# Two gate steps moved ahead of the first projections, and compressed scores in wider products

## The chip, the cores and the metric

The kernel runs on one core of one Trainium2 chip. The metric is the device time of one execution in microseconds (us). The kernel before takes 1661.98 us, the median of three runs (1661.27 to 1663.3).

## The reference, cut to what matters

The program computes a first block on 512 tokens of width 1024 and then two layers of a second block. The first block's attention is what the change touches. It has an mLSTM part (4 heads of 128) and a sparse attention part (8 heads of 64 in 2 groups), which are joined and multiplied by `w_out`.

```python
h = rms_norm(x, ln1_g)
mq, mk, mv, mo, mi, mf, aq, akc, avc, aks, avs, akw, avw, ag = split(h @ w_in)
# mLSTM: per head a row over the 512 tokens, from the two gate columns mi, mf
b = cumsum(log_sigmoid(mf + bias))          # a scan over the tokens
a = -b + (mi + bias)                        # then a running maximum of it
Wt = exp(D - m) * (q @ k.T);  hm = (Wt @ v) / max(|den|, exp(-m))
m_out = rms_norm(hm) * sigmoid(mo)
# sparse attention, branch 1 of 3: compressed keys, 32 per group
Kc, Vc = compress(akc), compress(avc)
p_c = softmax(q @ Kc.T - slope * dist);  o_c = p_c @ Vc
# branches 2 and 3: selected blocks and window, scores and values per head
a_out = g0 * o_c + g1 * o_s + g2 * o_w
x = x + concat(m_out, a_out) @ w_out
x = x + conv_ffn(rms_norm(x));  x = x + sigmoid(rms_norm(x) @ w_ple_gate) * (p @ w_ple_proj)
```

All of it is float32.

## The kernel before, in words

A float32 product is built from two reduced-precision parts of each operand, a high part (`whi`, `hh`) and a low part (`wlo`, `hl`). Three matmuls make one product: high by high, low by high, high by low (`mm`, lines 173 to 175). ScalarE (ACT) casts the high part of a weight tile (`split_w`, line 137). GpSimd (POOL) or VectorE (DVE) subtracts it from the raw tile to get the low part (lines 147 and 140). Activations are split likewise by `split`: ACT in line 201, DVE in line 202. SyncE (SP) issues the weight DMAs into `wraw` (line 157).

The first block's attention is written as a list of steps, `B1_ORDER`. `b1_attention` runs through it and emits each step's instructions. A scheduler then places them, and each engine runs its own queue in that order. The steps that matter here are:

- `B0`, `B1` (`b1_blocks`): key and value blocks for the compression. `v` (`b1_v`): values and gate columns (`gi`, line 784), 96 matmuls of 288 columns.
- `g` (`b1_gates`): 8 transposes of `gi` on TensorE (PE, line 663) and two biased copies on ACT (line 664) make the two gate rows, 4 partitions by 512 tokens.
- `R` (`b1_mlstm_rows`, lines 924 to 960): from these rows a chain over DVE and ACT: minimum (929), exp and log (930, 931), subtract (932), scan (934), subtract (937), scan with maximum (938), add (939), exp (940), a high part `m8` (945), and 4 transposes of the result on PE (line 954). Exp and log are in different activation tables, so that ACT loads a table in between (`ACT_TABLE_LOAD`).
- `Q` (`b1_mlstm_qk`): a projection with 24 matmuls of 512 columns; `k` and `q` are two and one more of these. `O` and `V`: mLSTM output gate (`mo`) and values. `M` (`b1_mlstm_head`): one mLSTM head, which ends in 4 transposes of `num` (line 1070).
- `S` (`b1_cmp_scores`): compressed scores of one group, for 4 token tiles and 4 heads. For each it has two matmuls of 32 columns, one with the high and one with the low part of the compressed keys `kc`, summed in one PSUM bank: 32 matmuls (line 838). One DVE addition of the bias (line 841) empties the bank, and the softmax follows.
- `A`, `P`, `E`: scores (line 878), transposes (901), values (907, 916) of the sparse heads.
- `u` (`b1_pT`): loads and transposes the second input (`praw`, line 632). `w` splits the first two mLSTM heads' outputs, and `W` (`b1_out`) multiplies them by their rows of `w_out`.

PSUM banks come from small pools. Projections, `S` and the transposes of `g` and `R` use the pool `psd`, which has two banks.

Of the kernel before, what the change touches and what calls it, by code (L numbers as in the profile page):

```python
# [9 lines left out]
OP = mybir.AluOpType  # L10
# [5 lines left out]
NT = 4  # L16
# [12 lines left out]
def sub(t, part, npart, off, dims):  # L29

    pitch = t.ap[0][0]
    return bass.AP(tensor=t.tensor, offset=t.offset + part * pitch + off,
                   ap=[[pitch, npart]] + [list(d) for d in dims])
# [7 lines left out]
class Build:  # L41
# [402 lines left out]

    B1_SIZES = dict(k=13, v=1, pa=6, pb=2, mp=6, p2=3, f=2, mf=2, ms=2)
    B1_D = (7,)
    B1_ORDER = "C B0 v B1 Q11 k q0 q1 Q00 X0 X1 g A00 O0 Y0 V0 A10 P00 Y1 S0 A01 A02 Q01 R M0 P01 P02 T0 A03 P03 A12 q2 E0 A11 P10 A13 P11 P12 P13 A30 E1 A20 P20 A21 P21 O1 q3 A22 A23 P22 Q10 A60 P23 V1 E2 A31 S1 P30 P31 A32 T1 A33 P32 M1 c Q21 A40 A42 Q20 P33 u E3 P40 A41 P41 A43 Q30 P42 A50 P43 w E4 W0 A52 P50 A51 P51 P52 A53 P53 A61 E5 A62 Q31 W1 P60 P61 M2 M3 A70 A63 P70 P62 P63 A72 U0 A71 A73 P71 P72 P73 U1 E6 E7"

    def b1_attention(self, ctx, h, first):
        self.c1 = self.pool(ctx, "const1", 1)  # L450
# [4 lines left out]
        self.aT, mT, x = [None] * 4, [None] * 4, {}  # L455
        for step in self.B1_ORDER.split():
            n = [int(c) for c in step[1:]]
# [366 lines left out]
    def b1_cmp_scores(self, g):  # L824

        nc, a = self.nc, self.a
        cbias = self.T("f", [128, NT, 128], name="cbias")
        nc.sync.dma_start(cbias, a["c_cbias"][g])
        pc = self.T("f", [128, NT, 128], name="pcx")
        mn = self.smallE([128, NT, 4], "cmn")  # L830
        ls = self.smallE([128, NT, 4], "cls")
        s = self.bankD()
        for i in range(NT):
            for r in range(4):
                hd = 4 * g + r
                lhs = self.qs[hd // 2][:, hd % 2, i * 128:(i + 1) * 128]
                for p in range(2):
                    nc.tensor.matmul(s[:, i * 128 + r * 32:i * 128 + r * 32 + 32], lhs,
                                     self.kc[:, p, 32 * g:32 * g + 32], start=(p == 0), stop=(p == 1))
        pf = pc.rearrange("p i (r n) -> p i r n", r=4)  # L840
        nc.vector.tensor_tensor(pc, s.rearrange("p (i n) -> p i n", i=NT), cbias, op=OP.add)
        nc.vector.tensor_reduce(mn, pf, axis=AX.X, op=OP.min)
        nc.vector.tensor_tensor(pf, sub(mn, 0, 128, 0, [[4, NT], [1, 4], [0, 32]]), pf, op=OP.subtract)
        nc.scalar.activation(pc, pc, AF.Exp)
        nc.vector.tensor_reduce(ls, pf, axis=AX.X, op=OP.add)
        nc.vector.reciprocal(ls, ls)
        nc.vector.tensor_tensor(ls, ls, sub(self.gate, 0, 128, 12 * g, [[24, NT], [3, 4]]), op=OP.mult)
        nc.vector.tensor_tensor(ls, ls, sub(self.rmask, 0, 128, 0, [[1, NT], [0, 4]]), op=OP.mult)
        nc.vector.tensor_tensor(pf, pf, sub(ls, 0, 128, 0, [[4, NT], [1, 4], [0, 32]]), op=OP.mult)
        return pc  # L850
# [937 lines left out]
```

## Time and profile before

| | us |
|---|---|
| median of 3 runs | 1661.98 |
| profiled execution | 1657.95 |
| its span (first to last instruction) | 1656.2 |
| PE busy / weight loads (PEld) | 1561.4 / 1385.7 |
| DVE / ACT / POOL busy | 943.6 / 756.2 / 546.9 |

The first block's attention lies between 20 and 335 us of the span; the rest is its dense part and the second block, which the change does not touch. PE is busy for 94% of the span, and the mean granted clock of TensorE is 0.98. The clock is told per stretch as a share of its upper level, 2.4 GHz; 0.50 is the lower one, 1.2 GHz. In such a table a busy time is followed by the number of instructions in brackets. A matmul's own time includes its way through the array, so that successive matmuls overlap: their spacing is read from the starts.

### The profile page before, as it was taken

How to read it: one execution, taken by the hardware profiler on the slowest of the kernel's cores; microseconds unless marked ns; L12 is line 12 of the kernel's file. 1: busy time of each engine (PE TensorE's matmuls, PEld its weight loads, DVE VectorE, ACT ScalarE, POOL GpSimd, SP SyncE). 2: the span in 40 equal slices, each digit the busy share in tenths (PEclk: the TensorE clock that was granted, in tenths of full speed). 3: DMA queues.
4: the chain of work that ended last, by engine and by line, in shares of the span. 5: the costliest groups of instructions: out<-in, count | busy, mean ns of one | idle time of the engine just before them, and what ended most of it. 6: DMA issues, size and time to landing. Idle time of an engine off the chain costs nothing.

```text
span 1656.2 us, 25923 instructions
## 1 busy us (share of the span) xinstructions
PE 1561.4 (94%) x9702; PEld 1385.7 (84%) x9702; DVE 943.6 (57%) x2090; ACT 756.2 (46%) x1703; POOL 546.9 (33%) x721
## 2 busy tenths in 40 slices
PE   6999998899999999898999999999989998999997
PEld 5899977778888888688899899998788786988785
DVE  4386667754454334646865558535447748566453
ACT  4465656743333323534554546533425545554432
POOL 4663533131111112347433243011666430431022
PEclk9999999999999999989999999999999999999999
DMA  5532222454333333322132144135322231333252
GB/s 173 139 103 68 65 77 83 161 179 153 100 89 101 103 105 112 104 75 65 39 83 69 54 124 121 40 120 164 115 61 64 78 90 38 102 111 93 73 182 76
DMA packets 189377, 163.61 MB, mean 99 GB/s; under 512 B 9664, under 2 KB 161312, under 8 KB 189252
## 3 DMA queue, kind: packets, MB, share of 16 engines
q1 hardware_dynamic: 189252, 161.96, 32.6%
q8 instruction: 76, 1.25, 0.3%
q14 instruction: 49, 0.40, 0.1%
HBM read 139.19 MB, written 12.58 MB: 92 GB/s over the span
## 4 chain that ended last, share of the span: by engine, by line
PE 72%; DVE 11%; DMA 5%; POOL 4%; ACT 4%; issue 3%; SPq 0%; POOLq 0%; DVEq 0%; ACTq 0%
PE psd L173 13%; PE psd L174 13%; PE psd L175 13%; PE pss L173 7%; PE pss L174 6%; PE pss L175 6%; POOL wlo L147 2%; DMA wraw<-in_w_in_dram 2%; ACT whi L137 2%; PE pss L1432 1%; PE pso L1469 1%; PE pst L1457 1%; DVE pt L202 1%; PE pss L1570 1%; DMA wraw<-in_w_out_dram 1%
## 5 line engine op out<-in xcount | busy, mean ns | idle before, releaser
L147 POOL TENSOR_TENSOR wlo<-wraw,whi 128x256 fp32r<-128x256 f32 (+1 forms) x432 | 320.7, 773 | 345.2 <-ACT whi L137 326.6
L137 ACT CAST whi<-wraw 128x1024 fp32r<-128x1024 f32 (+2 forms) x215 | 210.9, 981 | 332.0 <-PE pss L174 78.9
L173 PE MATMUL psd<-hh,whi 128*128 128x264 f32 (+2 forms) x1016 | 339.0, 335 | 2.9 <-DVE pT L202 1.2
L174 PE MATMUL psd<-hl,whi 128*128 128x264 f32 (+2 forms) x1016 | 338.5, 333 | 0.0
L175 PE MATMUL psd<-hh,wlo 128*128 128x264 f32 (+2 forms) x1016 | 337.2, 332 | 0.5 <-DVE wlo L140 0.5
L140 DVE TENSOR_TENSOR wlo<-wraw,whi 128x1024 fp32r<-128x1024 f32 (+1 forms) x106 | 116.0, 1094 | 189.5 <-ACT whi L137 189.2
L173 PEld LDWEIGHTS psd<-hh,whi 128*128 128x128 f32 x1016 | 192.6, 190 | 22.3 <-DVE pT L202 1.6
L175 PEld LDWEIGHTS psd<-hh,wlo 128*128 128x128 f32 x1016 | 192.7, 190 | 17.7 <-DVE wlo L140 1.0
L174 PEld LDWEIGHTS psd<-hl,whi 128*128 128x128 f32 x1016 | 192.8, 190 | 16.7
L173 PE MATMUL psd<-whi,hh 128*128 128x256 f32 (+1 forms) x480 | 140.2, 293 | 16.3 <-DVE va L202 11.3
L175 PE MATMUL psd<-whi,hl 128*128 128x256 f32 (+1 forms) x480 | 138.1, 288 | 0.0
L174 PE MATMUL psd<-wlo,hh 128*128 128x256 f32 (+1 forms) x480 | 138.0, 289 | 0.0
L173 PEld LDWEIGHTS psd<-whi,hh 128*128 128x128 f32 x480 | 92.8, 194 | 18.9 <-DVE va L202 12.2
L330 POOL TENSOR_TENSOR y<-x,g 128x512 f32<-128x512 f32 (+1 forms) x34 | 46.8, 1390 | 141.1 <-DVE x L522 102.1
L174 PEld LDWEIGHTS psd<-wlo,hh 128*128 128x128 f32 x480 | 93.0, 194 | 0.1
L175 PEld LDWEIGHTS psd<-whi,hl 128*128 128x128 f32 x480 | 93.0, 194 | 0.1
L201 ACT CAST pt<-pst 128x512 fp32r<-128x512 f32 (+3 forms) x130 | 63.7, 505 | 64.2 <-PE pst L1457 51.0
L202 DVE TENSOR_TENSOR pt<-pst,pt 128x512 fp32r<-128x512 f32 (+3 forms) x130 | 74.8, 582 | 22.8 <-ACT pt L201 22.1
L1115 POOL TENSOR_TENSOR act<-conv,act 128x512 fp32r<-128x512 f32 x16 | 25.4, 1588 | 163.6 <-ACT act L1114 163.6
L1441 ACT ACTIVATE pr<-pss,gls 128x528 f32<-128x528 f32 (+1 forms) x66 | 46.2, 700 | 47.7 <-DVE gls L1440 46.1
L1440 DVE TENSOR_REDUCE gls<-pss 128x1 f32<-128x528 f32 (+1 forms) x66 | 46.4, 703 | 37.4 <-PE pss L1432 36.6
L175 PE MATMUL pss<-hh,wlo 128*128 128x512 f32 x160 | 63.3, 396 | 0.0
(468 smaller groups left out, 3628.6 us busy)
## 6 DMA issues: line engine op xcount, KB each, us to landing
wraw<-in_w_in_dram SPq DMA_DIRECT2D x108, 512.0 KB
wraw<-in_w_up_dram SPq DMA_DIRECT2D x32, 512.0 KB
wraw<-in_w_out_dram SPq DMA_DIRECT2D x24, 512.0 KB
wraw<-in_w_down_dram SPq DMA_DIRECT2D x16, 512.0 KB
nbias<-in_na_bias_dram SPq DMA_DIRECT2D x16, 408.0 KB
k<-k SPq DMA_DIRECT2D x16, 296.0 KB
wraw<-in_w_ple_gate_dram SPq DMA_DIRECT2D x8, 512.0 KB
x_mid<-x SPq DMA_DIRECT2D x8, 512.0 KB
```

The costliest lines, as they stand in the source:

```text
L137: nc.scalar.copy(hi, raw)
L140: nc.vector.tensor_sub(lo, raw, hi.bitcast(F32))
L147: nc.gpsimd.tensor_sub(lo[:, p[0], p[1]], raw[:, p[0], p[1]], hi[:, p[0], p[1]].bitcast(F32))
L173: m(ps, A[0], B[0], start=start, stop=False)
L174: m(ps, A[0], B[1], start=False, stop=False)
L175: m(ps, A[1], B[0], start=False, stop=stop)
L201: nc.scalar.copy(hi, src)
L202: nc.vector.tensor_sub(lo, src, hi.bitcast(F32))
L330: self.nc.gpsimd.tensor_tensor(y[:n, c], x[:, c], g[:n, c], op=OP.mult)
L1115: nc.gpsimd.tensor_sub(lo, u, hi.bitcast(F32))
L1440: nc.vector.tensor_reduce(mx, sv, axis=AX.XY, op=OP.max, negate=True)
L1441: nc.scalar.activation(pr.rearrange("p (a n) -> p a n", a=2), sv, AF.Exp, bias=mx, accum_out=l)
```

## The change

`B1_ORDER` is another list, and `b1_cmp_scores` is written differently. Of the list, in the order of the new one:

- `g` and `R` stand before and after `B1`, right behind `v` and ahead of the projection `Q11`; they stood behind `X1` and behind `Q01`.
- `u` stands behind `A41`, not ahead of `E3`.
- `M2` stands behind `A50`, `M3` behind `P53`; both stood behind `P61`.
- `w` stands behind `A51`, `W0` behind `A53`, `W1` behind `P61`; they stood around `E4` and behind `Q31`. `Q31` stands behind `P50`.

A group's compressed scores become 16 matmuls of 64 columns in two banks, 8 in each. Both key parts lie side by side in the columns, and nothing is summed in PSUM. DVE adds the two halves: four additions of 256 columns (two per bank) in place of one of 512.

```diff
--- before.py
+++ after.py
@@ -444,7 +444,7 @@
 
     B1_SIZES = dict(k=13, v=1, pa=6, pb=2, mp=6, p2=3, f=2, mf=2, ms=2)
     B1_D = (7,)
-    B1_ORDER = "C B0 v B1 Q11 k q0 q1 Q00 X0 X1 g A00 ... S0 A01 A02 Q01 R M0 ... P33 u E3 P40 A41 P41 A43 Q30 P42 A50 P43 w E4 W0 A52 P50 A51 P51 P52 A53 P53 A61 E5 A62 Q31 W1 P60 P61 M2 M3 A70 ..."
+    B1_ORDER = "C B0 v g B1 R Q11 k q0 q1 Q00 X0 X1 A00 ... S0 A01 A02 Q01 M0 ... P33 E3 P40 A41 u P41 A43 Q30 P42 A50 M2 P43 E4 A52 P50 Q31 A51 w P51 P52 A53 W0 P53 M3 A61 E5 A62 P60 P61 W1 A70 ..."
 
     def b1_attention(self, ctx, h, first):
         self.c1 = self.pool(ctx, "const1", 1)
@@ -829,16 +829,19 @@
         pc = self.T("f", [128, NT, 128], name="pcx")
         mn = self.smallE([128, NT, 4], "cmn")
         ls = self.smallE([128, NT, 4], "cls")
-        s = self.bankD()
-        for i in range(NT):
-            for r in range(4):
-                hd = 4 * g + r
-                lhs = self.qs[hd // 2][:, hd % 2, i * 128:(i + 1) * 128]
-                for p in range(2):
-                    nc.tensor.matmul(s[:, i * 128 + r * 32:i * 128 + r * 32 + 32], lhs,
-                                     self.kc[:, p, 32 * g:32 * g + 32], start=(p == 0), stop=(p == 1))
+        rows = lambda t, b: t[:, 2 * b:2 * b + 2].rearrange("p i (r n) -> p (i r) n", r=4)
+        for b in range(2):
+
+            s = self.bankD()
+            for j in range(8):
+                i, hd = 2 * b + j // 4, 4 * g + j % 4
+                nc.tensor.matmul(s[:, 64 * j:64 * j + 64].rearrange("p (q n) -> p q n", q=2),
+                                 self.qs[hd // 2][:, hd % 2, i * 128:(i + 1) * 128],
+                                 self.kc[:, :, 32 * g:32 * g + 32], start=True, stop=True)
+            sv = s.rearrange("p (j q n) -> p j q n", j=8, q=2)
+            nc.vector.tensor_tensor(rows(pc, b), sv[:, :, 0], rows(cbias, b), op=OP.add)
+            nc.vector.tensor_tensor(rows(pc, b), sv[:, :, 1], rows(pc, b), op=OP.add)
         pf = pc.rearrange("p i (r n) -> p i r n", r=4)
-        nc.vector.tensor_tensor(pc, s.rearrange("p (i n) -> p i n", i=NT), cbias, op=OP.add)
         nc.vector.tensor_reduce(mn, pf, axis=AX.X, op=OP.min)
         nc.vector.tensor_tensor(pf, sub(mn, 0, 128, 0, [[4, NT], [1, 4], [0, 32]]), pf, op=OP.subtract)
         nc.scalar.activation(pc, pc, AF.Exp)
```

How the change moves instructions is seen in each engine's queue. A row gives the line, the operation, out<-in and the size, xN for repeats, and in brackets the engines or queues it waits for. Behind line 850 a line number of the changed kernel is 3 higher than before.

First PE's queue of the kernel before at the end of `v`, whose last matmuls write `psd` from `whi` and `hl`. Line 686 transposes a position table (`per`) for `B1`, and `hh`, `whi` with 512 columns is the projection `Q11`.

```order
L173 MATMUL psd<-whi,hh 128x288
L174 MATMUL psd<-wlo,hh 128x288
L175 MATMUL psd<-whi,hl 128x288
L686 MATMUL psd<-ident,per 128x128 [waits DMAHW3_49,DVE_49]
L173 MATMUL psd<-hh,whi 128x512 [waits DVE_49,Activation_49]
L174 MATMUL psd<-hl,whi 128x512
```

The same place of PE's queue in the changed kernel:

```order
L175 MATMUL psd<-whi,hl 128x288
L663 MATMUL psd<-ident,gi 4x128 [waits DVE_49]
L663 MATMUL psd<-ident,gi 4x128 x2
L663 MATMUL psd<-ident,gi 4x128 [waits Activation_49]
L663 MATMUL psd<-ident,gi 4x128 [waits DVE_49]
L663 MATMUL psd<-ident,gi 4x128 x3
L686 MATMUL psd<-ident,per 128x128 [waits DMAHW3_49,Activation_49]
L957 MATMUL psd<-ident,rows 128x128 [waits PE_49,Activation_49]
L957 MATMUL psd<-ident,rows 128x128 x3
L173 MATMUL psd<-hh,whi 128x512
L174 MATMUL psd<-hl,whi 128x512
```

The first transposes of the gate columns and the last ones of the finished rows now both stand between `v` and `Q11`.

ACT's queue of the changed kernel behind `v`: `cx` is the split of `B1`'s blocks, `lf` and `m` belong to `R`, `whi` is a weight tile of the coming projections.

```order
L664 ACTIVATE mif<-psd,gbias 4x512 [waits PE_49]
L201 CAST cx<-cxg 128x4x32 [waits DVE_49]
L201 CAST cx<-cxg 128x4x32 x3
L954 CAST onehot<-ohraw 128x4 [waits DMAHW5_49]
L201 CAST cx<-cxg 128x4x32 [waits DVE_49]
L201 CAST cx<-cxg 128x4x32 x3
L933 ACTIVATE lf_610<-lf_610 4x512 [waits DVE_49]
L137 CAST whi<-wraw 128x1024 [waits DMAHW6_49,Activation_49,Pool_49]
L934 ACT_TABLE_LOAD
L934 ACTIVATE lf_610<-lf_610 4x512 [waits Activation_49]
L948 CAST m_622<-mM 4x512 [waits DVE_49]
L943 ACT_TABLE_LOAD
```

The steps of `R` stand one behind the other here, with one weight cast among them, and both table loads with them.

PE's queue of the kernel before around the first group's compressed scores (line 838), with the sparse heads' scores (878) and transposes (901) and the projection `Q01` behind them:

```order
L838 MATMUL psd<-kc,qs 128x32 [waits DMAHW5_49]
L838 MATMUL psd<-kc,qs 128x32 x25
L878 MATMUL pss_1819<-k,qs 128x384 [waits DVE_49]
L878 MATMUL pss_1824<-k,qs 128x512 [waits DVE_49]
L901 MATMUL pst<-ident,sb 128x128 [waits DVE_49,PE_49]
L173 MATMUL psd<-hh,whi 128x512 [waits DVE_49]
```

In the changed kernel:

```order
L838 MATMUL psd<-kc,qs 128x64 [waits DMAHW6_49]
L838 MATMUL psd<-kc,qs 128x64 x4
L904 MATMUL pst<-ident,sb 128x128 [waits DVE_49,PE_49]
L881 MATMUL pss_1896<-k,qs 128x128 [waits DVE_49]
L881 MATMUL pss_1901<-k,qs 128x256 [waits DVE_49]
L838 MATMUL psd<-kc,qs 128x64 [waits DVE_49,PE_49]
L838 MATMUL psd<-kc,qs 128x64 x7
L904 MATMUL pst<-ident,sb 128x128 [waits DVE_49]
L173 MATMUL psd<-hh,whi 128x512 [waits DVE_49]
```

The second half now waits for DVE, and so does `Q01` behind it: both halves and `Q01` stand in the same one of the two `psd` banks, while the other is held by `Y1`, the compressed values.

## Rows read from the trace of the kernel before

**Rows 1.** The chain of waits that ended last, by engine.

```profile
PE 72%; DVE 11%; DMA 5%; POOL 4%; ACT 4%; issue 3%; SPq 0%; POOLq 0%; DVEq 0%; ACTq 0%
```

**Rows 2.** Busy table, most of the stage: stretch, PE, PEld, DVE, ACT, POOL, clock, DMA.

```profile
50.00:350.00 300.00, 280.33 (x1712) 247.31 (x1711) 194.72 (x561) 172.91 (x471) 122.03 (x171) 0.95 0.35 109
```

**Rows 3.** Timeline of PE behind step v: start, length, instruction, idle before and releaser.

```profile
47.74 0.27 PE L686 MATMUL psd<-ident,per 128*128 128x128 f32 x1
48.37 0.47 PE L173 MATMUL psd<-hh,whi 128*128 128x512 f32 x1 [0.36 <-DVE pet L688]
```

**Rows 4.** Timeline of ACT, same place.

```profile
48.37 0.15 ACT L784 COPY gi<-psd 128x8 f32<-128x8 f32 x1
...
49.83 0.90 ACT L201 CAST cx<-cxg 128x128 fp32r<-128x128 f32 x4 [1.03 <-DVE cxg L695]
...
55.56 1.05 ACT L137 CAST whi<-wraw 128x1024 fp32r<-128x1024 f32 x1 [3.43 <-DMA wraw<-in_w_in_dram]
```

**Rows 5.** Timeline of DVE, same place.

```profile
48.26 2.93 DVE L695 TENSOR_TENSOR cxg<-ks,pet 128x512 f32<-128x512 f32 x2
...
52.08 3.77 DVE L202 TENSOR_TENSOR cx<-cxg,cx 128x128 fp32r<-128x128 f32 x8
```

**Rows 6.** Groups by line, 85 to 150 us: busy, mean ns, idle before.

```profile
L938 DVE TENSOR_TENSOR_SCAN mM<-rows 4x512 f32<-4x512 f32 x1 | 1.2, 1240 | 0.0
L937 DVE TENSOR_TENSOR rows<-rows,lfF 4x512 f32<-4x512 f32 x1 | 0.9, 936 | 0.0
L841 DVE TENSOR_TENSOR pcx<-psd,cbias 128x512 f32<-128x512 f32 x1 | 0.7, 691 | 0.0
L945 ACT CAST m<-mM 4x512 fp32r<-4x512 f32 x1 | 0.6, 618 | 2.8 <-DVE mM L938 2.8
```

**Rows 7.** Timeline of ACT around the table load of step R.

```profile
100.94 1.28 ACT L931 ACT_TABLE_LOAD   x1
102.23 0.63 ACT L931 ACTIVATE lf<-lf 4x512 f32<-4x512 f32 x1
102.88 1.28 ACT L359 ACT_TABLE_LOAD   x1
```

**Rows 8.** What PE waited for, 104 to 335 us: total, times, longest.

```profile
PE psm L1070 <- DVE num L1068: 5.8, 1, 5.8
PE psd L173 <- ACT mo L359: 2.3, 1, 2.3
PE psd L173 <- DVE mq L205: 1.3, 1, 1.3
PE psd L173 <- DVE pT L202: 1.2, 1, 1.2
PE pss L173 <- ACT cat L212: 1.2, 1, 1.2
...
PE psd L632 <- DMA praw<-in_p_dram: 0.9, 1, 0.9
PE psd L173 <- ACT k L212: 0.9, 1, 0.9
```

**Rows 9.** Busy table, stretches of low clock.

```profile
104.00:108.00 4.00, 3.33 (x16) 3.33 (x17) 4.00 (x9) 1.81 (x7) 2.35 (x4) 0.57 0.46 131
131.00:137.00 6.00, 6.00 (x29) 5.60 (x29) 5.42 (x14) 1.78 (x8) 2.41 (x3) 0.56 0.57 169
330.00:336.00 6.00, 3.97 (x11) 2.96 (x12) 4.12 (x10) 3.70 (x7) 0.04 (x1) 0.50 0.84 329
```

**Rows 10.** Timeline of PE, 64-column matmuls and the first compressed scores.

```profile
127.50 0.27 PE L174 MATMUL psd<-w,grep 128*128 128x64 f32 x1
127.61 0.28 PE L175 MATMUL psd<-w,grep 128*128 128x64 f32 x1
...
129.03 4.56 PE L838 MATMUL psd<-kc,qs 128*128 128x32 f32 x32
```

More of the change, by code (lines that the diff above doesn't have):

```diff
@@ L446 @@
     B1_D = (7,)
-    B1_ORDER = "C B0 v B1 Q11 k q0 q1 Q00 X0 X1 g A00 O0 Y0 V0 A10 P00 Y1 S0 A01 A02 Q01 R M0 P01 P02 T0 A03 P03 A12 q2 E0 A11 P10 A13 P11 P12 P13 A30 E1 A20 P20 A21 P21 O1 q3 A22 A23 P22 Q10 A60 P23 V1 E2 A31 S1 P30 P31 A32 T1 A33 P32 M1 c Q21 A40 A42 Q20 P33 u E3 P40 A41 P41 A43 Q30 P42 A50 P43 w E4 W0 A52 P50 A51 P51 P52 A53 P53 A61 E5 A62 Q31 W1 P60 P61 M2 M3 A70 A63 P70 P62 P63 A72 U0 A71 A73 P71 P72 P73 U1 E6 E7"
+    B1_ORDER = "C B0 v g B1 R Q11 k q0 q1 Q00 X0 X1 A00 O0 Y0 V0 A10 P00 Y1 S0 A01 A02 Q01 M0 P01 P02 T0 A03 P03 A12 q2 E0 A11 P10 A13 P11 P12 P13 A30 E1 A20 P20 A21 P21 O1 q3 A22 A23 P22 Q10 A60 P23 V1 E2 A31 S1 P30 P31 A32 T1 A33 P32 M1 c Q21 A40 A42 Q20 P33 E3 P40 A41 u P41 A43 Q30 P42 A50 M2 P43 E4 A52 P50 Q31 A51 w P51 P52 A53 W0 P53 M3 A61 E5 A62 P60 P61 W1 A70 A63 P70 P62 P63 A72 U0 A71 A73 P71 P72 P73 U1 E6 E7"
     def b1_attention(self, ctx, h, first):
```

## The prediction

> **What bounds the kernel now.** I read the chain of waits first: 72% of it is PE and 11% DVE [rows 1]. So an edit is worth what it does to PE's queue, and an engine beside PE counts only where PE waits for it. The busy table then shows where PE is not full. From 50 to 350 us, most of the first block's attention, PE is busy for 280.33 of 300 us at a mean granted clock of 0.95 [rows 2]. That leaves 19.7 us of idle time and up to 15 us (5% of 300) lost to low clock, and all that a new order can win lies in these two. PE's waits name the places: 5.8 us for the last head's `num` in front of the dense part, 2.3 for `mo`, 1.3 and 0.9 around `W0` (`mq`, `k`), 1.2 and 0.9 in step `u` (`pT`, `praw`), 1.2 for `cat` [rows 8]. Behind or around such places the clock is at about half [rows 9]. Of the gate steps that are moved, little shows as a wait: their chain over DVE and ACT runs beside projections that keep PE busy. That is the point on which the forecast turns: before, the chain has cover; now PE stands in it.
>
> The sum is made against the profiled execution, 1657.95 us, which is 4.03 below the median of 1661.98. What comes out is added to the median.
>
> **g and R ahead of Q11.** PE executes its queue in the written order, and the four transposes of the finished rows now stand ahead of `Q11`. They need the last exp of the chain. So all of `g` and `R` is a wait of PE, with the projection and all behind it. Before, `Q11` starts at 48.37 us [rows 3]. The walk from there, with an estimated 0.1 us for a hand-over and durations from the rows:
>
> - The last `gi` copy on ACT ends at 48.52 (48.37 + 0.15) [rows 4]. Five transposes (four of the second row, the last of the first) at 0.11 spacing [rows 10] and one run through the array (0.27 as for `per` [rows 3]) bring PE to 49.3. The two biased copies on ACT are of the 4 by 512 kind. The eleven of that kind on the path take from 618 to 1240 ns, first and last in [rows 6], and add to 8.8 us. Two of the short ones bring ACT to 50.6.
> - DVE has the two `cxg` additions in its queue ahead of the first step of `R`: 2.93 us [rows 5], from about 50.3, since their `per` transpose stands behind those of `gi`. They end at 53.35, and the minimum at 54.05.
> - ACT: exp to 54.9; a `whi` cast of 1.05 [rows 4] stands ahead of the table load, to 56.0 (its weights landed at 55.56 before, which fits); table load 1.28 [rows 7], to 57.3; log to 57.95. Meanwhile DVE does the eight `cx` subtractions, 3.77 us [rows 5], to about 58.5.
> - DVE: subtract to 58.8, scan to 60.05, subtract 0.94 to 61.0, scan 1.24 to 62.2 [rows 6]. ACT: `m8` 0.62 [rows 6] to 62.85, the second table load 1.28 [rows 7] to 64.15 (it stands behind `m8`, so nothing hides it), exp to 64.8. PE: four transposes to 65.35.
>
> `Q11` starts 17.0 us later. If the hand-overs overlap as closely as neighbours on one engine do, 1.5 us less; with 0.25 us at each of twelve, about 3 more: 15.5 to 20. Nothing wins it back later as far as I see: the next five projections are PE's own work, and weights that are ready earlier don't shorten it.
>
> PE restarts at low clock. Between 104 and 108 us, behind the 2.3 us wait, PE is busy for 3.33 us at 0.57 [rows 9]; at full clock that is 1.90, so 1.4 is lost. Between 330 and 336, behind the longest wait, 3.97 at 0.50 loses 2.0. Between the two: +1.7.
>
> What goes at the old places: the wait for `pet`, 0.36 [rows 3], since `per` is ready long before; the wait for `mo`, 2.3 [rows 8], which ends late because ACT loads two tables just ahead of it [rows 7], and with it the 1.4 of low clock; twelve transposes at 0.11 [rows 10], 1.3. Together -5.4. Net of this part: 17.0 + 1.7 - 5.4 = +13.3.
>
> The Trainium skill weighs on one term. Its page "ScalarE: Activation LUTs", section "What ACT_TABLE_LOAD costs", gives about 1283 ns for the load and another 1380 ns of drain for each switch of set. The trace has the 1.28 us but not the drain: the log starts at 102.23, 0.01 us after the load ends at 102.22. By the page two switches would add 2.8 us to the stall and the forecast would be 1673.0; I go by the rows.
>
> **Compressed scores.** 32 matmuls take 4.56 us [rows 10], 0.1425 each; 16 take 2.3, so -2.3 a group. From 131 to 137 us, around the first group, PE is busy all 6.00 us, at 0.56 [rows 9]: 2.6 us (6.00 x 0.44) of low clock. If the clock stayed up, a group would give -4.9. Against it: PE's queue shows the second half and `Q01` behind it waiting for DVE, since both halves and `Q01` use one bank. An addition of 512 columns took 0.69 [rows 6]; the two waits cost up to 1.4. If a further clock fall comes with them (1.4 as above), a group costs +0.5 with the saved matmuls, or +2.8 if these were hidden anyway. I take -2.3 + 1.4 = -0.9 a group, -1.8 in all, from -9.8 to +5.6.
>
> **u later.** Its transposes of `praw` stand closer together, and the loads come through two buffers. The waits seen were 0.9 for the load and 1.2 for `pT` [rows 8]. Two such pairs at most are new: 0 to +4.2, and I take +2.5, a little over one pair, because the matmuls that stood between the transposes are what moved away.
>
> **w and W0 later.** The waits for `k` and `mq`, 0.9 + 1.3 [rows 8], go, because other matmuls now stand between the split and the product: -2.2. With the low clock behind them (1.4) it could be -3.6, or 0 if the new place has its own wait.
>
> **M2, M3 and the end.** Before, PE ends its work and waits 5.8 for `num` and 1.2 for `cat` [rows 8], 7.0 in all, then runs 2.0 us worth of low clock. Now twelve matmuls of 512 columns stand behind the last head's products, ahead of its transposes. Each takes between 0.11 [rows 10] and 0.47 [rows 3]; at 0.3 they cover 3.6 us: -3.6. Its bounds are 0 (the head is simply as late) and -9.0 (waits and clock all gone).
>
> **Sum.** 13.3 - 1.8 + 2.5 - 2.2 - 3.6 = +8.2: 1666.2 for the profiled execution, 1670.2 for the median.
>
> **Rivals.**
> - *The clock stays up.* A cause outside the counted work: PE at its upper level through `S`, `W0`, the restart and the end. Then each group gives -4.9 (8.0 better), the restart costs nothing (1.7 better), the end and `W0` gain 2.0 and 1.4: 13.1 in all, +8.2 becomes -4.9, 1657.1, faster. It decides once 11.5 of the 13.1 come (8.2 + 3.3); at 8.2 it makes no change. For it: all these stretches have low clock now, and fewer waits stand in them. Against: a 17 us wait is just what preceded the low clock in two of the three rows.
> - *The chain is paid back.* The eleven operations (8.8 us) leave a stretch in which DVE was busy for 4.00 of 4.00 us [rows 9]. If DVE and ACT set the pace from there to the first scores, all of it comes back: -0.6, 1661.4, no change. Against: in those rows PE is the one that is full wherever it does not wait for `mo`, which is already counted.
> - *The banks decide.* Both groups cost +2.8 and `u` its full 4.2: +9.1 on the sum, 1679.3. For it: one bank serves both halves and the projection.
> - *The wait is not there*, because PE's matmuls don't stand behind the rows' transposes on the chip. Then 18.7 go from the sum: -10.5, 1651.5. No row shows a matmul that starts ahead of a waiting one.
>
> **How the numbers follow.** The forecast has 0.42, the clock 0.17, the pay-back 0.20, the banks 0.15, no wait 0.06. A difference under 0.2% (3.3 us) can't be told from none here. So faster 0.23, same 0.20, slower 0.57. The range of 8 in 10 goes from 1655, which takes in most of the clock's case and leaves out the missing wait, to 1679, which leaves out half of the banks' case; the forecast's own range is 1666 to 1675.
>
> **What would show it.** In the profile after: PE idle for 15 to 20 us behind the 96 matmuls of `v`, released by ACT, with both table loads within the gap; then a clock near 0.5 for some 3 us. No wait for `mo` at `O0`. Twice 8 matmuls of 64 columns for each group, the second 8 released by DVE. Waits for `praw` of 2 us or more together. The wait for `num` at 2 to 3 us. I am wrong in the main point if `Q11` starts before 60 us, and wrong in the sum if the gap is there and the time is still below 1662: then the stretch from `Q11` to the dense part must be at least 17 us shorter, and the table of busy time and clock will say by which of the two.

## The result and the profile after

The changed kernel takes 1688.01 us, the median of four runs (1683.11 to 1690.39), against 1661.62 for the kernel before beside it. The ratio is 1.0163, 95% interval [1.0145, 1.0181]: slower by 26.4 us, where +8.2 was forecast and 1679 was the end of the range.

The wait that the forecast turns on is there. PE's timeline behind step `v` in the changed kernel, to set beside [rows 3] (start, length, instruction, idle time before it and its releaser):

```profile
49.03 0.27 PE L686 MATMUL psd<-ident,per 128*128 128x128 f32 x1
64.50 1.12 PE L957 MATMUL psd<-ident,rows 128*128 128x128 f32 x4 [15.19 <-ACT rows L943]
65.27 0.78 PE L173 MATMUL psd<-hh,whi 128*128 128x512 f32 x1
65.84 0.63 PE L174 MATMUL psd<-hl,whi 128*128 128x512 f32 x1
```

`Q11` starts at 65.27 in place of 48.37, 16.9 us later. ACT's timeline of the same stretch shows the chain that holds it; [rows 4, 7] are its counterparts:

```profile
54.00 1.03 ACT L137 CAST whi<-wraw 128x1024 fp32r<-128x1024 f32 x1
55.05 1.28 ACT L934 ACT_TABLE_LOAD   x1
56.34 0.63 ACT L934 ACTIVATE lf<-lf 4x512 f32<-4x512 f32 x1
61.89 0.62 ACT L948 CAST m<-mM 4x512 fp32r<-4x512 f32 x1 [4.92 <-DVE mM L941]
62.52 1.28 ACT L943 ACT_TABLE_LOAD   x1
63.82 0.63 ACT L943 ACTIVATE rows<-lfF 4x512 f32<-4x512 f32 x1
```

Both loads stand in the gap, and ACT goes on 0.01 and 0.02 us after each. The Trainium skill's page "ScalarE: Activation LUTs", section "What ACT_TABLE_LOAD costs", adds a drain of about 1380 ns to each switch. These rows show none, as [rows 7] did not.

The busy table of the stretch (PE, PEld, DVE, ACT, POOL, clock, DMA), before first, gives what PE loses:

```profile
48.00:70.00 22.00, 21.14 (x91) 16.81 (x91) 10.51 (x17) 9.71 (x22) 17.45 (x24) 1.00 0.50 134
```

```profile
48.00:70.00 22.00, 6.26 (x21) 4.94 (x21) 12.23 (x22) 9.25 (x19) 12.07 (x12) 0.62 0.26 73
```

The spacing of the matmuls is 0.43 until 70.1 us and 0.23 from there:

```profile
69.68 0.62 PE L174 MATMUL psd<-hl,whi 128*128 128x512 f32 x1
70.11 0.43 PE L175 MATMUL psd<-hh,wlo 128*128 128x512 f32 x1
70.61 0.39 PE L174 MATMUL psd<-hl,whi 128*128 128x512 f32 x1
70.84 0.39 PE L175 MATMUL psd<-hh,wlo 128*128 128x512 f32 x1
```

So the first 4.8 us of `Q11` run at the lower clock. Its first eleven matmuls take 4.84 us in place of 2.6 and lose 2.3.

What PE waited for from 40 to 370 us in the changed kernel; [rows 8] are the counterparts:

```profile
PE psd L957 <- ACT rows L943: 15.2, 1, 15.2
PE pst L904 <- DVE sb L901: 2.7, 5, 1.7
PE psd L173 <- DVE xw L500: 2.3, 2, 1.5
PE pst L904 <- DVE pt L202: 2.3, 2, 2.1
PE pso L910 <- DVE pt L202: 2.1, 4, 1.1
PE psm L1073 <- DVE num L1071: 2.0, 1, 2.0
...
PE pss L173 <- ACT cat L212: 1.2, 1, 1.2
```

The waits for `mo` and for `mq` and `k` around `W0` are gone and the one for `num` fell from 5.8 to 2.0, as the sum had it. In their place stand many waits for DVE (`sb`, `pt`, `xw`).

Two numbers cut the loss in two. The dense part's first matmul, before and then in the changed kernel:

```profile
333.20 0.79 PE L173 MATMUL pss<-whi,cat 128*128 128x512 f32 x1 [1.19 <-ACT cat L212]
```

```profile
353.38 0.73 PE L173 MATMUL pss<-whi,cat 128*128 128x512 f32 x1 [1.19 <-ACT cat L212]
```

It starts 20.2 us later. What follows, the dense part and the second block, took 1323.0 us (1656.2 - 333.2) and takes 1335.2 (1688.6 - 353.4): 12.2 more, in code that no line of the change touches. No term of the sum is about this part. The start varies between executions, though: in four runs whose queues are alike up to the dense part and beyond (before, and experiments 4, 8 and 13 below) it was 333.2, 331.4, 336.6 and 335.1. A single profile's shift of 4 us there proves nothing. The rest was 1323.0 and 1323.1 in the two profiles in which the whole program is alike, but it is not that steady everywhere: in experiments 6, 9, 11 and 14, whose instructions stand in the same order in the second block, it runs from 1321.1 to 1326.3. What a part costs is therefore read from the medians below, and the profiles only say where.

### The profile page after: what moved, and what is told of

The parts are those of the page before. It is cut to its first block, busy times and chain, and to the rows that moved or that the text cites. A ratio compares the mean times of both kernels' runs of the same rounds, so it can differ in the third digit from the quotient of the medians.

```text
span 1688.6 us, 25870 instructions
## 1 busy us (share of the span) xinstructions
PE 1573.6 (93%) x9670; PEld 1391.0 (82%) x9670; DVE 947.7 (56%) x2096; ACT 758.5 (45%) x1703; POOL 553.0 (33%) x721
## 5 line engine op out<-in xcount | busy, mean ns | idle before, releaser
L147 POOL TENSOR_TENSOR wlo<-wraw,whi 128x256 fp32r<-128x256 f32 (+1 forms) x432 | 326.1, 787 | 385.4 <-ACT whi L137 384.9
L174 PE MATMUL pss<-hl,whi 128*128 128x512 f32 x160 | 63.3, 396 | 0.0
```

The lines of the kernel that those rows point to most:

```text
L147: nc.gpsimd.tensor_sub(lo[:, p[0], p[1]], raw[:, p[0], p[1]], hi[:, p[0], p[1]].bitcast(F32))
L174: m(ps, A[0], B[1], start=False, stop=False)
```

## The experiments

Each is compared with the kernel before, run beside it on the same chip. "Start" is the start of the dense part in the profile, "rest" what follows it to the end of the span. The ratio is to its own runs of the kernel before, whose medians lie between 1659.0 and 1661.6; start and rest are from one profile each.

| run | median us | ratio, 95% interval | start | rest |
|---|---|---|---|---|
| before (first profile) | 1661.6 | | 333.2 | 1323.0 |
| changed | 1688.0 | 1.0163 [1.0145, 1.0181] | 353.4 | 1335.2 |
| 1 g and R early | 1669.3 | 1.0063 [1.0043, 1.0082] | 341.9 | 1323.7 |
| 2 scores alone | 1671.1 | 1.0066 [1.0042, 1.0090] | 333.3 | 1336.9 |
| 3 late steps alone | 1665.1 | 1.0038 [1.0024, 1.0053] | 338.4 | 1323.9 |
| 4 rotation +2 alone | 1668.4 | 1.0053 [1.0032, 1.0074] | 331.4 | 1331.4 |
| 5 changed, rotation restored | 1676.0 | 1.0107 [1.0092, 1.0123] | 350.6 | 1328.1 |
| 6 rows early, transposes late | 1657.4 | 0.9982 [0.9968, 0.9997] | 329.2 | 1326.2 |
| 7 heads alone | 1664.1 | 1.0027 [1.0015, 1.0040] | 337.4 | 1324.0 |
| 8 output product alone | 1660.7 | 1.0004 [0.9994, 1.0014] | 336.6 | 1323.1 |
| 9 changed, both losses out | 1665.9 | 1.0042 [1.0026, 1.0058] | 336.6 | 1321.1 |
| 10 scores on top of 6 | 1661.2 | 1.0015 [1.0006, 1.0024] | 336.3 | 1325.1 |
| 11 heads and output product | 1658.6 | 0.9997 [0.9983, 1.0010] | 333.0 | 1326.3 |
| 12 u alone | 1657.4 | 0.9991 [0.9982, 1.0000] | 334.8 | 1321.1 |
| 13 rotation +1 alone | 1664.9 | 1.0028 [1.0014, 1.0041] | 335.1 | 1329.0 |
| 14 as 6, u late | 1659.2 | 0.9989 [0.9979, 0.9999] | 336.2 | 1323.9 |
| 15 before, no residual | 1660.9 | 1.0002 [0.9990, 1.0013] | 335.9 | 1324.1 |
| 16 late steps, no residual | 1657.9 | 0.9988 [0.9972, 1.0004] | 337.1 | 1320.5 |
| 17 late steps, xw elsewhere | 1664.5 | 1.0021 [1.0009, 1.0033] | 339.7 | 1325.8 |
| 18 as 17, rows as in 6 | 1658.4 | 0.9990 [0.9980, 1.0000] | 334.1 | 1323.2 |

**The three parts, one at a time.** Order lists against that of the kernel before; experiment 2 has the new `b1_cmp_scores` and the old list.

```text
 1: "C B0 v g B1 R Q11 ... X1 A00 ... Q01 M0 ..."
 3: "... P33 E3 P40 A41 u P41 ... A50 M2 P43 E4 A52 P50 Q31 A51 w P51 P52 A53 W0 P53 M3 ... P61 W1 ..."
```

> The kernel before with only g and R moved behind v and B1; scores, heads and output product as before. Theory A (the stall): PE waits about 15 us for the last exp of the rows ahead of Q11, restarts at low clock, and gets back only the wait for mo and the transposes: the dense part starts about 12 us later than before, and the time is +10 to +14 us (1672 to 1676). Rival B (the stall is paid back, the loss of the changed kernel comes from its other parts): dense part within 4 us of before, time within 4 us.

> Only the compressed scores in 64-column products over two banks, order list as before. Theory A (bank rotation): up to the dense part the gain and the wait for DVE cancel, -1 to +3 us; but two more calls for a psd bank shift which calls of the second block get the third pool (every third call does), its queues are laid out otherwise, and it gets 6 to 12 us longer with no line of it changed: 1667 to 1676 in all. Rival B (the later loss is only the low clock that follows from another start time): the second block takes the same time as before within 3 us, and the total is within 3 us of before.

> Only u, w, W0, W1, M2, M3 and Q31 moved, as in the changed kernel; g, R and the scores as before. Theory A (output product between the heads): W0's new place makes DVE wait for the loads of xw and PE for DVE, which costs more than the old waits, and the earlier last head gives some 4 us at the end: dense part +3 to +6 us later, second block unchanged, 1664 to 1669. Rival B (the blind sum: -2.2 for W0, +2.5 for u, -3.6 at the end): 3 us faster, 1658 to 1660.

Measured against 1659.67: +9.7, +11.4 and +5.4 us, which adds to 26.5; the change cost 26.4. So the parts explain it by themselves. In their profiles, the first has the wait of 15.2 us and nothing lost in the rest (1323.7). The second starts its dense part with before (333.3) and loses 13.9 us behind it. The third has nothing lost in the rest either (1323.9).

**Why the scores cost time in the second block.** Every PSUM bank of the pool `psd` comes from `bankD`, which counts its calls; where a third pool is open, every third call takes a bank from it.

```python
self.nd += 1
pool = self.ps_e if self.ps_e and self.nd % 3 == 0 else self.ps_d
```

Two groups with two banks in place of one raise the count by 2 for all that follows. Experiment 4 does only that, to the kernel before; 13 takes the third phase, and 5 gives the changed kernel its old phase back.

```diff
         self.dense = True
+        self.nd += 2      # 4;  += 1 in 13, and in 5 on the changed kernel
```

> The kernel before with the counter of bank calls raised by 2 where the dense part begins: no instruction is added, removed or moved in the first block's attention. Theory A (bank rotation): the second block is laid out as in the changed kernel and gets 6 to 12 us longer: 1667 to 1674. Rival B (clock and start time): nothing changes, 1660 to 1664, since nothing starts later.

> The kernel before with the counter of bank calls raised by 1 (not 2) where the dense part begins: the third of the three possible rotations, first block untouched. Theory A (the rotation of the kernel before is merely the best of three): 1664 to 1672. Rival H (only the shift by 2 is bad): 1657 to 1662.

> The changed kernel with the counter of bank calls raised by 1 where the dense part begins, so that with the two extra calls of the scores it stands where it did modulo 3. Theory A (bank rotation): the second block gets its old layout back and 7 to 11 us: 1676 to 1681, with the dense part starting as late as in the changed kernel. Rival B (what follows the first block is slower by the clock and the later start): 1685 to 1690 as the changed kernel.

Raised by 2, the rest takes 1331.4 and the run 8.7 us more; by 1, 1329.0 and 4.6 more, just inside what was expected. Restored in the changed kernel, its ratio falls from 1.0163 to 1.0107, some 9 us, and its median by 12, to 1676.0 (the profile is of its slowest run, 1680.5; there the rest is 1328.1). Its attention stays late (the start is at 350.6). The queues of experiment 4 are row for row those of the kernel before until the second block. The second block's two layers each have a product of `mix`, whose first matmul marks how far PE has come. Before, and then in experiment 4:

```profile
1140.11 0.39 PE L173 MATMUL pss<-whi,mix 128*128 128x512 f32 x1
1600.71 0.39 PE L173 MATMUL pss<-whi,mix 128*128 128x512 f32 x1
```

```profile
1140.59 0.39 PE L173 MATMUL pss<-whi,mix 128*128 128x512 f32 x1
1607.36 0.39 PE L173 MATMUL pss<-whi,mix 128*128 128x512 f32 x1
```

Counted from the start of the dense part, the first comes 2.3 us later (809.2 against 806.9), the second 8.4 later (1275.9 against 1267.5). So some 2 us are lost in the first layer and 6 in the second. In the first layer, the busy tables around 900 us, before first, then experiment 4:

```profile
895.00:935.00 40.00, 34.29 (x265) 30.93 (x264) 24.38 (x55) 18.50 (x45) 7.44 (x12) 1.00 0.12 29
```

```profile
890.00:930.00 40.00, 33.24 (x215) 29.61 (x214) 25.04 (x56) 15.64 (x41) 1.69 (x4) 0.83 0.12 29
```

In 40 us PE does 215 matmuls in place of 265, at a clock of 0.83 in place of 1.00; part of that is work that stands elsewhere in the new order. PE's waits there, of experiment 4 (888 to 932 us) and then of the changed kernel (910 to 955 us), name the same new wait:

```profile
PE psd L1306 <- DVE z L1406: 1.9, 1, 1.9
```

```profile
PE psd L1308 <- DVE z L1408: 1.9, 1, 1.9
```

Before, there is none for `z` in this stretch. In the second layer no single wait carries the loss. Between the two products of `mix`, one wait for `pr` grows and one for `rx` is new (the first row is before, the others are experiment 4), while others shrink:

```profile
PE pss L1432 <- ACT pr L1441: 3.1, 4, 1.4
```

```profile
PE pss L1433 <- ACT pr L1442: 5.2, 5, 1.4
PE psd L173 <- DVE rx L1339: 1.8, 1, 1.8
```

So another bank for a call means another order of the queues of the second block, and that order costs 8.7 us, in several places. The rival that a later start alone would do it fell: experiment 4 starts no later. The scores alone (experiment 2) cost 2.7 us more than the rotation alone; the intervals of the two overlap.

**Is it the place of the transposes or the chain?** Experiment 6 cuts `R` in two: the chain stays early, the transposes and the copies behind them become a step `r` at R's old place.

```diff
-"... v B1 Q11 ... X1 g A00 ... Q01 R M0 ..."
+"... v g B1 R Q11 ... X1 A00 ... Q01 r M0 ..."
```

> g and R early as in the first experiment, but the four transposes of the finished rows (and the copies behind them) stay at R's old place behind Q01. Theory A (only PE's place in the order stalls): no wait of 15 us, Q11 starts within 2 us of before, the wait for mo is gone; dense part 0 to 5 us earlier, 1655 to 1661. Rival C (the chain itself, by standing ahead of weight casts on ACT, holds the projections): PE waits for whi or wlo around 55 to 66 us and most of the 9.7 us stays, 1665 to 1670.

1657.4 us, 0.18% faster than before [0.03, 0.32] and 11.9 us faster than experiment 1. PE's timeline, of experiment 6:

```profile
49.01 0.27 PE L687 MATMUL psd<-ident,per 128*128 128x128 f32 x1
49.55 0.50 PE L173 MATMUL psd<-hh,whi 128*128 128x512 f32 x1 [0.27 <-DVE pet L689]
62.12 0.50 PE L173 MATMUL psd<-hh,whi 128*128 128x512 f32 x1 [1.11 <-DVE mq L202]
```

`Q11` starts at 49.55. Its other waits up to 145 us are small (1.5 for `k`, 1.4 for `pt`), and none is for `mo`. So it was PE's place in the order, and rival C fell. DVE waits 5.2 us for the loads of `xw` here (240 to 352 us) and 0.6 before, in the fastest kernel of all; that bears on the next question.

**What of the late steps costs?** Single parts: M2, M3, Q31; w, W0, W1; both; u.

> Only M2, M3 and Q31 moved; u, w, W0, W1 at their old places. Theory A (W0's new place is the loss): the wait for num at the end shrinks by some 4 us and nothing replaces it: 1654 to 1659. Rival D (two more heads among the scores of heads 4 to 6 overfill DVE there): PE waits for DVE between 255 and 300 us and the time is 1663 to 1667.

> Only w, W0 and W1 moved; heads, u and Q31 at their old places. Theory A: DVE's wait for the xw loads and PE's wait for DVE appear as in the changed kernel around W0 and W1, dense part 4 to 9 us later: 1664 to 1669. Rival D: W0 alone does no harm (within 3 us of before, or faster by the 2.2 us of the old waits).

> M2, M3, Q31 and w, W0, W1 moved, u at its old place; the heads alone cost 3.3 us, w, W0 and W1 alone leave every queue as it was. Theory A (W0 behind the heads waits for the xw loads): dense part 4 to 7 us later than before with DVE waits for xw: 1663 to 1668. Rival G (u's new place is what delays the loads, since praw and xw share two buffers): no more than the heads alone, 1661 to 1665, and no wait for xw over 1 us.

> Only u moved behind A41. Theory A (as in the blind sum): two pairs of waits for praw and pT, 0 to +4 us at the dense part: 1661 to 1665. Rival G: the loads of xw are pushed back as well, W0 waits, +4 to +7 us: 1665 to 1668.

The heads alone cost 0.27%, both together nothing, u nothing or a little gain; all of them 0.38%. They don't add. Experiment 8 is a lesson of its own: moving w, W0 and W1 in the list alone left every queue of all five engines row for row as before, since the scheduler puts them where it did. It tests nothing of the theory, and its 1.0004 [0.9994, 1.0014] is what the measurement makes of the same program. With all steps moved, DVE waits for the loads of `xw`; here before and then experiment 3, 240 to 352 us:

```profile
DVE xw L500 <- DMA xw<-in_x_dram: 0.6, 1, 0.6
```

```profile
DVE xw L500 <- DMA xw<-in_x_dram: 6.0, 4, 2.0
```

Experiments 15 and 16 leave the residual of `W` out of the computation (no load of `xw`, a copy in place of the addition); 17 does all the work, with `xw` from the pool of 13 buffers.

```diff
-            nc.sync.dma_start(x, a["x"][0, ts, c])           # 15, 16
-            nc.vector.tensor_add(x, x, d)                    # 15, 16
+            nc.vector.tensor_copy(x, d)                      # 15, 16
-            x = self.T("f", [128, S], name="xw")             # 17, 18
+            x = self.T("k", [128, S], name="xw")             # 17, 18
```

> The kernel before with step W leaving out the residual: xw is not loaded, DVE copies the product instead of adding it. All theories: W's waits in the kernel before were short (0.5 us), so within 3 us of before, 1656 to 1662. It is the base for the next run.

> The late steps moved as in the third experiment (u, w, W, M2, M3, Q31), and step W without the residual as in the run just above, so that no load of xw can hold DVE. Theory A (the loads of xw are the loss of the late steps): the difference to the run above is under 1.5 us. Rival D (DVE and PE are held by the heads themselves): the difference stays 4 to 6 us, and PE waits for mn, sb, aT and pt.

> The late steps moved as in the third experiment, all the work done; xw takes its buffers from the pool of 13 (k) and no longer shares two with praw and others. Theory A (xw's loads wait for buffers): the 5.4 us of the third experiment become -4 to 0: 1656 to 1660, DVE's waits for xw under 1 us. Rival D: 1662 to 1666.

Without the loads the late steps are 3.0 us faster than their base (1657.9 against 1660.9; the two intervals overlap). The sum gave them -3.3, but the likeness is luck: the largest gain in it was the wait for `num`, and in experiment 16 that is still 5.2 us. With the loads the late steps cost 5.4. Other buffers hardly help: experiment 17 still costs 0.21%, and DVE waits as long:

```profile
DVE xw L500 <- DMA xw<-in_x_dram: 6.3, 5, 2.5
```

So the shared buffers are not the cause. SP's timeline of experiment 3 shows what the loads stand behind (line 501 stores a finished piece, line 496 loads a later one):

```profile
285.85 1.47 SPq L501 DMA_DIRECT2D x_zero<-xw  x2
287.90 0.33 SPq L496 DMA_DIRECT2D xw<-in_x_dram  x1
...
291.63 0.33 SPq L501 DMA_DIRECT2D x_zero<-xw  x1
294.39 0.33 SPq L496 DMA_DIRECT2D xw<-in_x_dram  x1
```

Each load is issued behind a store, which waits for DVE's addition, which waits for a load. But the kernel before has stores and loads in the same turn, and there DVE waits 0.6 us:

```profile
286.86 0.33 SPq L501 DMA_DIRECT2D x_zero<-xw  x1
288.88 0.33 SPq L496 DMA_DIRECT2D xw<-in_x_dram  x1
```

Nor is the wait enough by itself. Experiment 18 below has the same late steps as 17, DVE waits as long and PE waits 4.6 us for DVE, and it is as fast as before (0.9990) and within 1.0 us of experiment 6:

```profile
DVE xw L501 <- DMA xw<-in_x_dram: 6.5, 4, 2.0
PE psd L173 <- DVE xw L501: 4.6, 4, 2.2
```

The queues of 16 also differ from those of 3 in more than the loads. So the cost of the late steps goes when the loads go, and goes when the rows come early as well. What makes it in experiment 3 stays open.

**Do the causes add, and is there a better version?** Experiment 9 is the changed kernel with the transposes at R's old place and the rotation restored. Experiment 10 is 6 with the wide scores and the rotation restored; 14 is 6 with u late; 18 is 17 with the rows of 6.

> The changed kernel with both named losses taken out: the transposes of the rows back at R's old place, and the counter of bank calls raised by 1 ahead of the dense part. Theory A (the losses add): the restored rotation alone gave 1676, and moving the transposes gave 12 us over the first experiment, so 1662 to 1667; what stays is the loss of the moved heads and u. Rival E (the parts interact, the stall also gave the engines behind PE time to run ahead): 1668 to 1676.

> The kernel before with g and R early but their transposes at R's old place, the compressed scores in 64-column products, and the counter raised by 1 ahead of the dense part; heads, u, w and W as before. Theory A: the scores add nothing up to the dense part, the second block keeps its layout: 1654 to 1659, like the rows alone (1657.4). Rival F (the two banks of the scores cost more when DVE has the rows' chain behind it, or the 64-column products pay now): 1660 to 1664, or 1650 to 1653.

> The kernel before with g and R early, their transposes at R's old place, and u behind A41; nothing else. Theory A (the two small gains add): 1654 to 1657.5. Rival I (u's 0.1% was noise or is eaten by another order): 1657.5 to 1661.

> The run just above with g and R early as well, their transposes at R's old place; scores as before. Theory A (the two gains add: -3 for the rows, -3 for the late steps): 1652 to 1656. Rival (they meet in the same DVE time): 1657 to 1660.

Experiment 9 falls from 1688.0 to 1665.9, as expected if the losses add (its profile is of its fastest run, 1659.5). What is left, 0.42%, was not taken apart. Experiment 10 is 0.33% behind experiment 6 (1.0015 against 0.9982): the wide scores gain nothing even with the rotation put right, and in that pair they lose. The order of the second block differs between the two as well, so whether the scores themselves lose is not shown. 14 and 18 are 0.1% faster than before, not better than 6. Experiment 6 is the fastest tried, by 0.18%, at the edge of what can be told.

## Why the prediction was wrong, point by point

**The wait: right.** 17.0 us were summed, 16.9 measured, and each step on the chain is within about 1 us (the log ended at 56.97, not 57.95; the exp at 64.45, not 64.8). The eight `cx` subtractions, which were to end at 58.5 and hold the next step, ended at 55.05 in DVE's timeline, ahead of the log, and held nothing. The low clock behind the wait lost 2.3, not 1.7. Net +13.3 was forecast and experiment 1 costs 9.7, with an interval of 7.1 to 13.6 that still holds 13.3. Some of the 8.8 us of the rival "the chain is paid back" may have come back; that any did is not shown, and not all of it did.

**Compressed scores: the term that failed worst.** -1.8 was taken, with +5.6 as the upper end; the edit costs 11.4 us. Up to the dense part the step was near: the saved matmuls are real (two rows of 8 matmuls of about 1.05 us in place of 4.56, [rows 10]), and the first group's second half waits for DVE as feared (1.4). PE's waits of experiment 2, 125 to 225 us:

```profile
PE pss L881 <- DVE mn L882: 1.7, 3, 0.8
PE psd L838 <- DVE ls L895: 1.4, 1, 1.4
PE pst L904 <- DVE sb L901: 1.2, 2, 0.9
```

Its dense part starts with that of before, as far as one profile can tell. The step that failed is one that the prediction never took: its sum ended where the dense part begins. The text ahead of it even says that the rest is not touched. The two extra calls of `bankD` change the queues of the second block in both layers, 8.7 us by experiment 4. The order of both kernels, compared to the end and not only around the edits, would have shown that the queues change, though not what that costs.

**w, W0, M2, M3 and the end: wrong in sign.** The sum had -2.2 and -3.6, and +2.5 for u: -3.3. Experiment 3 measured +5.4. The old waits for `k` and `mq` did go. The cover for `num` failed: it shrank to 2.0 in the changed kernel, but in the late steps alone (experiment 3, 240 to 352 us) PE waits as long as before, and new waits stand beside it:

```profile
PE psm L1070 <- DVE num L1068: 5.8, 1, 5.8
PE psd L173 <- DVE xw L500: 2.5, 2, 1.7
PE pso L907 <- DVE aT L922: 2.2, 1, 2.2
```

The prediction had let a wait at W0's new place cancel the gain, but not exceed it. Which of the new waits makes the 5.4 stays open, as said above. u alone costs nothing (0.9991), where +2.5 was taken, although its profile has 2.6 us of waits for `praw`.

**Rivals.** "The banks decide" named 1679.3. Both halves do use one bank and PE does wait 1.4 us between them, but its price (2.8 a group) does not show at the start of the dense part. "The clock stays up" fell: the mean clock is still 0.72 from 150 to 160 us and 0.74 from 220 to 240, behind the two groups. "The wait is not there" fell with the first rows above.

**The range.** Its upper end rested on bounds for places in the attention. The sum missed by 18.2 us (26.4 - 8.2): 13.2 for the scores (11.4 + 1.8), 8.7 for the late steps (5.4 + 3.3), and 3.6 the other way for the rows. Of the 13.2, the rotation is 8.7, and for that the range held nothing.

## What to carry to other kernels

Work that is off the critical path has cover only as long as no instruction of the critical engine stands behind it: move a chain early, but leave the critical engine's last use of it where it was (12 us here). Before an edit that asks for one more buffer or bank is called local, look for counters that deal out such things to later code, and compare the queues to the end of the program. A new wait in a profile is not yet a cost: look for a run that has the wait without the loss (here experiments 6 and 18).

## What the runs showed that was not expected

- The order of steps in the list is not the order on the engines: a list with three steps at other places gave the same queues (experiment 8).
- Three phases of one counter give 1661, 1665 and 1668 us with the first block's code untouched: the kernel before has the best of the three.
- The time from the start to the dense part varies by up to 5 us between executions of the same queues (331.4 to 336.6), and the rest by up to 5 as well where the order of the second block is the same (1321.1 to 1326.3), although two profiles agree to 0.1.
